# The input projection in float32 on unsplit operands, with a third weight buffer

## The chip, the cores and the metric

The kernel runs on one core of one Trainium2 chip. The metric is the device time of one execution in microseconds (us). The engines are TensorE (PE, with its weight loads shown as PEld), VectorE (DVE), ScalarE (ACT), GpSimd (POOL) and SyncE (SP), which issues most of the loads.

## The reference

One layer of a decoder computes 512 prompt tokens and a sample group of 8 x 4 tokens, 544 tokens in all, in float32:

```python
z = rms_norm(x, Wl['g_mix']) @ Wl['w_in']           # 1024 channels -> 3080 columns
za, zb, zc = jnp.split(z, [RWKV_COLS, RWKV_COLS + FOX_COLS], axis=-1)
ya, S, shift = rwkv7_mix(za, ...)                   # RWKV recurrence, 4 heads
q, k, v, logf = fox_project(zb, ...)                # FoX attention, 8 heads
yb = fox_fn(q, k, v, logf)
yc, conv_buf = conv_module(zc, ...)                 # 31 taps
x = x + jnp.concatenate([ya, yb, yc], axis=-1) @ Wl['w_out']
x = x + cross_attend(x, mk, mv, ...)
f, ffn_buf = conv_ffn(x, ffn0, ...)
x = x + f
```

The change concerns the first line, the input projection. The outputs are the new activations, the caches and the states.

## The kernel before

Activations lie with channels on the 128 partitions and the 544 tokens along a row, in eight blocks of 128 channels. A weight product takes a block of 128 output columns, a span of tokens (272, or 256 and 288 for the RWKV columns) and eight blocks k of the contraction, which add up in one bank of PSUM (`bank_g`, two of them).

Products take operands of type float32 or float32r, a type of the same size which keeps fewer digits. To keep the precision of float32 with float32r operands, each operand is split into a high and a low part, both float32r: `split` (L244) copies the high part on ACT (`w_hi`, L177) and takes the difference on DVE (`w_lo`, L247). `gemm_steps` (L306) then makes three products for each k: high x high, high weight x low activation, low weight x high activation. The activations are split once, where they come out of the first transposes (L481 and L482 make `act_h` and `act_l`); the weights are split block by block in `weights` (L267), just before use, with high priority.

Weights come through a pool of two slots (`wraw`, tile `w_raw`) of 2048 numbers on each partition, two blocks to a slot. SP issues the loads in order, each when its slot is free, which is when the split has read it. The same two slots take the first cached keys of the later attention, through GpSimd.

The stage has two parts. First come the eight blocks of RWKV columns, with the recurrence's gates beside them (`gates`, up to L673). Then `weave` (L1241) runs three streams side by side: the 17 other blocks (`fox_and_conv`: the forget gate, four of the convolution, twelve of FoX), the RWKV recurrence (`rwkv_recurrence`, ahead of the others by 800 instructions) and the convolution's taps (`conv_ahead`). `weave` takes the next step from the stream whose done share is least. A step of the projection counts `kb * n * 1.25e-3` of a total of 106, the recurrence counts to 79, the convolution to 84. When the projection ends, so does the weave; what is left of the other streams runs later beside the sample's attention. The recurrence ends with its sample steps (`sample_steps`), which load a state S (L971). Two pools of the stage close with the projection, and the attention's tiles take their place.

Of the kernel before, what the change touches and what calls it, by code (L numbers as in the profile page):

```python
# [43 lines left out]
def _consts():  # L44
    """What depends on shapes alone: identities, masks, selections."""
# [46 lines left out]
    # rows (head, page of four, query) against pages, queries and columns of the like  # L92
# [18 lines left out]
def _past_consts():  # L111
    """of rows (head, page of four, query): causal mask, selections of pages, queries and columns"""
# [14 lines left out]
def _cross_consts():  # L127
    """of rows (head of two, 64 of the keys, token) those of a head and the 64; then selections of 32 rows, four times over"""
    p, m = np.arange(128)[:, None], np.arange(8)[None, :]
    own = [(m // 4 == h) & (m % 4 == p // 32) for h in range(2)]  # L130
    four = [p == 32 * x + np.arange(128)[None, :] % 32 for x in range(4)]
    return np.concatenate(own + four, 1).astype(np.float32)
# [5 lines left out]
def _pack_vectors(x):  # L138
    """Per-channel vectors side by side, a column for each 128 channels."""
# [15 lines left out]
def hybrid_step(tc, A):  # L155
# [62 lines left out]
    def rsqrt_from(out, in_, scale, eps):  # L218
        """out = (in * scale + eps) ** -0.5 by the logarithm and the exponential"""
# [3 lines left out]
    def half_xyy(t, y, x, scale, eps):  # L223
        """t = (x * scale + eps) / 2 * y ** 2 for y, about the inverse root: (1.5 - t) * y is that root to the last bits"""
# [3 lines left out]
    def rsqrt_rows(out, x, n, scale, eps, eps_ap, work):  # L228
        """out = (x * scale + eps) ** -0.5 for n numbers to a partition"""
# [6 lines left out]
    def neg_sigmoid(t, e):  # L236
        """-1 / (1 + exp(-t)) in place, for t >= -40; by a Newton step"""
# [6 lines left out]
    def split(h, l, src, tt=vtt):  # L244
        """src = h + l exactly, both float32r"""
# [14 lines left out]

    wload = [nc.sync.dma_start]
# [5 lines left out]
    def weights(src, kb, cols, width=128, raws=None):  # L267
        """loads blocks of columns, two at most, and returns how to split each"""
# [13 lines left out]
        if raws is not None:  # L282
            raws.extend(parts)

# [21 lines left out]
    def gemm_steps(src, cols, xh, xl, evac, bank, spans=EVEN, kb=8, ahead=0, raws=None, first=None):  # L306
        """evac(ps, i, a) for span a of the i-th block of 128 columns; yields what each step costs TensorE"""
        for i0 in range(0, len(cols), at_once[0]):
            pair = cols[i0: i0 + at_once[0]]
            part = first if first and i0 == 0 else weights(src, kb, pair, raws=raws)  # L310
# [4 lines left out]
            for q, a in order:  # L315
                lo, n = spans[a]
                ps = bank()
                with tc.high_priority(ahead) if ahead else ExitStack():
                    for k in range(kb):
                        hv, lv = w[q](k)  # L320
# [3 lines left out]
                yield kb * n * 1.25e-3  # L324
# [1872 lines left out]
```

## Time and profile before

| | |
|---|---|
| time, median of 3 runs | 1304.64 us (1300.55 to 1308.29) |
| span of the profiled execution | 1301.6 us |
| PE, DVE, ACT, POOL busy | 95%, 62%, 39%, 22% of the span |
| the input projection's products | from 12.7 to 319.7 us |

Busy time is the time in which an engine has at least one instruction in flight. Products on PE are pipelined, so a busy PE is not PE at its peak. A row of a group gives a line of the kernel, engine, operation, output<-inputs, the shape, the number of instructions, their busy time and the mean duration of one, then the idle time of the engine just before them and what ended it. The granted clock is given as a share of 2.4 GHz.

### The profile page before, as it was taken

Reading aid. Unit: us, or ns where it says so; the run is one execution under the profiler, and the core shown is the slowest. Engines: PE = TensorE matmul, PEld = TensorE weight load, DVE = VectorE, ACT = ScalarE, POOL = GpSimd, SP = SyncE. Lnnn points to the kernel's source line nnn. Section 1 sums busy time; section 2 is a strip of 40 time slices with the busy share of each in tenths; the row PEclk is TensorE's granted clock in tenths of the full one; section 3 lists DMA queues with packets and bytes.
Section 4 is the critical chain, followed back from the end, with each engine's and each line's share of the span. In section 5 each row is a group of like instructions: output and inputs, shape, how many; then the busy total and the mean of one; then the engine's idle time right before and its main releaser. Section 6 shows DMA issues by size and latency. Waiting matters only on the chain.

```text
span 1301.6 us, 24852 instructions
## 1 busy us (share of the span) xinstructions
PE 1234.1 (95%) x10410; PEld 1011.6 (78%) x10410; DVE 809.1 (62%) x1514; ACT 501.2 (39%) x996; POOL 290.6 (22%) x322
## 2 busy tenths in 40 slices
PE   7899899999899999999998988999999999999997
PEld 6788788875555467654447875799999999999996
DVE  4699998765777377453234677557767424777631
ACT  5454543341456435221242422335444323444321
POOL 1262430033342131112223242012111100111120
PEclk9999999997699999999998998999999999999999
DMA  7221220221788497576663465033322323222231
GB/s 227 59 65 51 50 75 19 67 87 44 268 304 304 155 306 244 198 231 226 218 215 118 151 232 174 23 103 98 98 93 60 93 73 127 68 96 88 76 111 48
DMA packets 129649, 173.83 MB, mean 134 GB/s; under 512 B 7029, under 2 KB 110981, under 8 KB 121336
## 3 DMA queue, kind: packets, MB, share of 16 engines
q0 software_dynamic: 15216, 84.80, 18.1%
q1 hardware_dynamic: 88160, 70.76, 17.9%
q10 hardware_dynamic: 26160, 16.66, 4.4%
q8 instruction: 82, 1.34, 0.4%
q14 instruction: 31, 0.25, 0.1%
HBM read 164.54 MB, written 7.88 MB: 132 GB/s over the span
## 4 chain that ended last, share of the span: by engine, by line
PE 77%; DVE 9%; issue 5%; ACT 4%; DMA 3%; POOL 2%; SPq 0%; POOLq 0%; ACTq 0%; DVEq 0%
PE bank_g L186 42%; PE bank_r L186 10%; PE bank_d L186 6%; PE bank_s L186 6%; PE bank_v L186 4%; PE bank_a L186 2%; PE bank_r L216 2%; DVE w_lo L247 1%; PE bank_t L216 1%; PE bank_x L216 1%; DMA w_raw<-in_w_in_dram 1%; DMA w_raw<-in_w_out_dram 1%; DVE four L855 1%; DVE KT L1404 1%; ACT w_hi L177 1%
## 5 line engine op out<-in xcount | busy, mean ns | idle before, releaser
L186 PE MATMUL bank_g<-four,w_hi 128*128 128x272 f32 (+1 forms) x1536 | 284.7, 301 | 2.7 <-ACT w_hi L177 2.0
L177 ACT CAST w_hi<-w_raw 128x1024 fp32r<-128x1024 f32 (+3 forms) x149 | 140.6, 946 | 269.8 <-PE bank_g L186 206.1
L186 PEld LDWEIGHTS bank_g<-four,w_hi 128*128 128x128 f32 x1536 | 222.1, 189 | 26.4 <-issue 19.9
L247 DVE TENSOR_TENSOR w_lo<-w_raw,w_hi 128x1024 fp32r<-128x1024 f32 (+3 forms) x149 | 164.0, 1103 | 87.2 <-ACT w_hi L177 78.2
L186 PE MATMUL bank_g<-four,w_lo 128*128 128x272 f32 (+1 forms) x768 | 173.4, 301 | 0.5 <-DVE w_lo L247 0.5
L186 PEld LDWEIGHTS bank_g<-four,w_lo 128*128 128x128 f32 x768 | 122.1, 189 | 11.3 <-issue 8.6
L186 PE MATMUL bank_g<-act_h,w_hi 128*128 128x272 f32 (+2 forms) x400 | 124.6, 312 | 6.2 <-ACT w_hi L177 2.8
L186 PE MATMUL bank_g<-act_h,w_lo 128*128 128x272 f32 (+2 forms) x400 | 122.9, 308 | 0.0
L186 PE MATMUL bank_g<-act_l,w_hi 128*128 128x272 f32 (+2 forms) x400 | 122.0, 305 | 0.0
L2108 POOL TENSOR_SCALAR ysm<-HS,vec 128x32 f32<-128x32 f32 x44 | 42.0, 954 | 255.1 <-ACT HS L177 255.1
L1404 DVE STREAM_TRANSPOSE KT<-w_raw 128x2048 f32<-128x2048 f32 x32 | 73.5, 2302 | 23.9 <-PE bank_s L186 22.8
L186 PEld LDWEIGHTS bank_g<-act_h,w_hi 128*128 128x128 f32 x400 | 79.5, 199 | 10.5 <-ACT w_hi L177 3.2
L186 PEld LDWEIGHTS bank_g<-act_h,w_lo 128*128 128x128 f32 x400 | 79.1, 198 | 2.8 <-issue 1.2
L186 PEld LDWEIGHTS bank_g<-act_l,w_hi 128*128 128x128 f32 x400 | 79.4, 198 | 2.3 <-issue 1.1
L186 PE MATMUL bank_s<-KT,w_hi 128*32 128x128 f32 x1024 | 76.6, 292 | 3.4 <-DVE rsq L226 1.7
L186 PE MATMUL bank_d<-four,w_hi 128*128 128x272 f32 x384 | 78.1, 299 | 0.0
L186 PE MATMUL bank_g<-in_h,w_hi 128*128 128x272 f32 x352 | 73.6, 290 | 0.0
L186 PE MATMUL bank_g<-in_l,w_hi 128*128 128x272 f32 x352 | 73.5, 290 | 0.0
L186 PE MATMUL bank_g<-in_h,w_lo 128*128 128x272 f32 x352 | 73.2, 289 | 0.0
L186 PE MATMUL bank_v<-page,w_lo 128*32 128x512 f32 x256 | 67.8, 603 | 1.8 <-DMA page<-in_cache_fox_v_dram,kidx 1.8
L186 PEld LDWEIGHTS bank_s<-KT,w_hi 128*32 128x32 f32 x1024 | 39.2, 115 | 32.5 <-issue 19.8
L186 PEld LDWEIGHTS bank_d<-four,w_hi 128*128 128x128 f32 x384 | 61.9, 193 | 1.0
(631 smaller groups left out, 2458.6 us busy)
## 6 DMA issues: line engine op xcount, KB each, us to landing
w_raw<-in_w_up_dram SPq DMA_DIRECT2D x20, 1024.0 KB, 5.1
w_raw<-in_w_down_dram SPq DMA_DIRECT2D x16, 704.0 KB, 4.7
w_raw<-in_w_in_dram SPq DMA_DIRECT2D x17, 512.0 KB, 4.2
w_raw<-in_cache_mem_k_dram SPq DMA_DIRECT2D x16, 512.0 KB, 5.0
sV<-in_cache_mem_v_dram POOLq DMA_DIRECT2D x12, 512.0 KB, 6.4
w_raw<-in_w_in_dram SPq DMA_DIRECT2D x4, 1024.0 KB, 6.6
w_raw<-in_w_xk_dram ACTq DMA_DIRECT2D x8, 512.0 KB, 10.6
w_raw<-in_w_xv_dram ACTq DMA_DIRECT2D x8, 512.0 KB, 10.7
```

The costliest lines, as they stand in the source:

```text
L177: nc.scalar.copy(out, in_)
L186: pinned(nc.tensor.matmul(out, lhsT, rhs, start=start, stop=stop, skip_group_check=True))
L216: pinned(nc.tensor.transpose(out=out, in_=in_, identity=ident[p0:p0 + k, p0:p0 + k]))
L247: tt(out=l, in0=src, in1=h.bitcast(F32), op=SUB)
L855: vstt(out=yp, in0=U[:, m, w: w + SEQ], scalar=w_tap, in1=yp, op0=MUL, op1=ADD)
L1404: nc.vector.transpose(out=KT, in_=K)
L2108: nc.gpsimd.tensor_scalar(out=ysm, in0=H[:, 2:6, 1:], scalar1=w[2], scalar2=b, op0=MUL, op1=ADD)
```

## The change

The projection's operands are no longer split. `xh` holds the scaled activations once, as float32; half of the copies that fill it move from ACT to DVE. The tile `act_l` goes, and in its place a pool `wmore` adds a third slot to the rotation of weight slots for this stage. `weights` hands out the raw tile, and `gemm_steps` makes one float32 product for each k when there is no low activation. The planner counts such a step 1.67e-3 for each k and column in place of 1.25e-3; the totals in `weave` stay. All other weight products remain split. The rest of the diff removes comments and moves the class `Slots` up.

```diff
+    class Slots:
+        def __init__(self, *pools):
+            self.turns, self.n = [p for p, k in pools for _ in range(k)], -1
+        def tile(self, *args, **kw):
+            self.n += 1
+            return self.turns[self.n % len(self.turns)].tile(*args, **kw)
...
-    def weights(src, kb, cols, width=128, raws=None):
+    def weights(src, kb, cols, width=128, raws=None, whole=False):
...
+        if whole:
+            return lambda i: lambda k: (parts[i][:, k],)
...
-            part = first if first and i0 == 0 else weights(src, kb, pair, raws=raws)
+            part = first if first and i0 == 0 else weights(src, kb, pair, raws=raws, whole=xl is None)
...
                     for k in range(kb):
+                        if xl is None:
+                            mm(ps[:, :n], w[q](k)[0], xh[k][:, lo: lo + n], k == 0, k == kb - 1)
+                            continue
                         hv, lv = w[q](k)
...
-                yield kb * n * 1.25e-3
+                yield kb * n * (1.25e-3 if xl else 1.67e-3)
...
-    xh, xl = (acts.tile([128, 8, NT], F32R, name=n) for n in ("act_h", "act_l"))
+    wslot[0] = Slots((wraw, 2), (pool("wmore", 1, axs), 1))
+    xh = acts.tile([128, 8, NT], F32, name="act")
...
-            early = weights(A["w_in"][0], 8, [m * 128 for m in order_z[:2]])
+            early = weights(A["w_in"][0], 8, [m * 128 for m in order_z[:2]], whole=True)
...
-                h, l = xh[:, m, lo: lo + n], xl[:, m, lo: lo + n]
-                act(out=h, in_=p, func=AF.Copy, scale=V("g_mix", m))
-                vstt(out=l, in0=p, scalar=V("g_mix", m), in1=h.bitcast(F32), op0=MUL, op1=SUB)
+                if m % 2:
+                    vts(out=xh[:, m, lo: lo + n], in0=p, scalar1=V("g_mix", m), scalar2=None, op0=MUL)
+                else:
+                    act(out=xh[:, m, lo: lo + n], in_=p, func=AF.Copy, scale=V("g_mix", m))
...
-    for step in gemm_steps(w_in, [m * 128 for m in order_z], blocks(xh), blocks(xl), evac_z, gb, spans=((0, 256), (256, 288)), first=early):
+    for step in gemm_steps(w_in, [m * 128 for m in order_z], blocks(xh), None, evac_z, gb, spans=((0, 256), (256, 288)), first=early):
...
     def fox_and_conv():
-        x = blocks(xh), blocks(xl)
+        x = blocks(xh), None
...
     axs.close()
+    wslot[0] = wraw
```

## Rows read from the trace of the kernel before

**Rows 1.** The page: busy time by engine, and the granted clock in 40 slices.

```profile
PE 1234.1 (95%) x10410; PEld 1011.6 (78%) x10410; DVE 809.1 (62%) x1514; ACT 501.2 (39%) x996; POOL 290.6 (22%) x322
...
PEclk9999999997699999999998998999999999999999
```

**Rows 2.** Busy time by engine and stretch; the last three are clock, DMA, GB/s.

```profile
core 0: us, PE busy (x) PEld busy (x) DVE busy (x) ACT busy (x) POOL busy (x), PEclk, DMA share, GB/s
12.00:62.00 50.00, 44.48 (x300) 40.92 (x300) 30.64 (x60) 22.95 (x43) 9.58 (x18) 0.97 0.39 117
62.00:178.00 116.00, 105.58 (x810) 97.20 (x810) 111.25 (x193) 58.65 (x86) 51.09 (x51) 0.96 0.25 64
178.00:250.00 72.00, 71.76 (x1179) 60.89 (x1179) 60.29 (x151) 24.95 (x64) 6.24 (x8) 1.00 0.11 31
250.00:320.00 70.00, 69.71 (x568) 51.00 (x565) 40.43 (x93) 24.64 (x57) 18.63 (x19) 0.90 0.23 63
```

**Rows 3.** Groups by line, 12 to 320 us: one pass's products, weight loads.

```profile
L186 PE MATMUL bank_g<-act_h,w_hi 128*128 128x272 f32 (+2 forms) x400 | 124.6, 312 | 6.2 <-ACT w_hi L177 2.8 <-DVE fsq L816 1.3 <-DVE zS L565 1.0
...
L186 PEld LDWEIGHTS bank_g<-act_h,w_hi 128*128 128x128 f32 x400 | 79.5, 199 | 10.5 <-ACT w_hi L177 3.2 <-issue 2.1 <-DVE fsq L816 1.2
```

**Rows 4.** Timeline: start, length; first and last of 43 back-to-back float32r products.

```profile
275.73 0.29 PE L186 MATMUL bank_g<-act_h,w_lo 128*128 128x272 f32 x1
...
281.01 0.29 PE L186 MATMUL bank_g<-act_h,w_lo 128*128 128x272 f32 x1
```

**Rows 5.** Chain of waits, 12 to 320 us, shares by line.

```profile
by line: PE bank_g L186 26.9%; PE bank_r L186 25.9%; DVE w_lo L247 4.0%; issue 3.5%; PE bank_x L216 3.0%; DVE four L855 3.0%; PE bank_r L216 2.8%; PE bank_x L186 2.0%; DVE Dr L954 1.9%; DVE later L523 1.6%; DVE zb L575 1.2%; DVE zb L576 1.1
```

**Rows 6.** Timeline: a float32r product, then four records of float32 products.

```profile
264.73 0.29 PE L186 MATMUL bank_g<-act_h,w_lo 128*128 128x272 f32 x1
264.85 1.08 PE L186 MATMUL bank_x<-fsq,cf 128*128 128x272 f32 x4
```

**Rows 7.** Groups by line, 62 to 178 us: products of one pass.

```profile
L186 PE MATMUL bank_g<-act_h,w_hi 128*128 128x272 f32 (+2 forms) x205 | 62.4, 304 | 3.4 <-DVE fsq L816 1.3 <-DVE zS L565 1.0 <-DVE X L955 0.4
```

**Rows 8.** Groups by line: the splits up to 320 us, then 62 to 178.

```profile
L177 ACT CAST w_hi<-w_raw 128x1024 fp32r<-128x1024 f32 x25 | 26.1, 1046 | 33.2 <-PE bank_g L186 32.4 <-DMA w_raw<-in_w_in_dram 0.8
...
L247 DVE TENSOR_TENSOR w_lo<-w_raw,w_hi 128x1024 fp32r<-128x1024 f32 x25 | 31.7, 1271 | 3.5 <-ACT w_hi L177 3.5
...
L247 DVE TENSOR_TENSOR w_lo<-w_raw,w_hi 128x1024 fp32r<-128x1024 f32 x13 | 17.1, 1318 | 0.0
```

**Rows 9.** PE's waits, 12 to 320 us: total, times, longest.

```profile
PE bank_x L186 <- DVE ft L226: 3.6, 1, 3.6
PE bank_g L186 <- ACT w_hi L177: 2.8, 1, 2.8
```

**Rows 10.** Busy time and clock, columns as in rows 2: the dips.

```profile
155.00:160.00 5.00, 1.74 (x11) 1.13 (x9) 5.00 (x8) 2.93 (x7) 3.58 (x2) 0.88 0.00 0
160.00:165.00 5.00, 4.67 (x18) 4.43 (x19) 5.00 (x10) 3.36 (x7) 2.61 (x3) 0.50 0.00 0
305.00:310.00 5.00, 5.00 (x14) 1.50 (x9) 1.59 (x6) 0.22 (x2) 0.99 (x1) 0.50 0.18 41
```

**Rows 11.** The same at 400 to 450 us, and its first group on PE.

```profile
400.00:450.00 50.00, 49.45 (x359) 25.69 (x359) 27.67 (x73) 26.72 (x80) 11.15 (x11) 1.00 0.65 233
...
L186 PE MATMUL bank_s<-KT,w_hi 128*32 128x128 f32 x138 | 12.0, 281 | 0.0
```

**Rows 12.** The low activations: durations in ns, smallest, median, largest.

```profile
L482 DVE SCALAR_TENSOR_TENSOR act_l<-bank_r,vec,act_h x8: 474/495/518, 8.6 to 22.2; 128x256 fp32r<-128x256 f32 x4, 128x288 fp32r<-128x288 f32 x4
```

**Rows 13.** The page's loads of the projection's weights; timeline of SP's queue.

```profile
w_raw<-in_w_in_dram SPq DMA_DIRECT2D x17, 512.0 KB, 4.2
...
254.53 1.83 SPq L971 DMA_DIRECT2D S<-in_state_rwkv_dram  x2
```

**Rows 14.** Timeline: first and last products of the recurrence's sample steps on PE.

```profile
281.23 1.15 PE L186 MATMUL bank_r<-ident,S 64*64 64x64 f32 x32
...
312.62 0.48 PE L216 MATMUL bank_r<-ident,y 128*128 128x128 f32 x1
```

More of the change, by code (lines that the diff above doesn't have):

```diff
@@ L1615, in normed @@
         vstt(out=l, in0=xTs[m // 4][:, m % 4, s], scalar=V("g_x", m), in1=h.bitcast(F32), op0=MUL, op1=SUB)
-    class Slots:
-        def __init__(self, *pools):
-            self.turns, self.n = [p for p, k in pools for _ in range(k)], -1
-        def tile(self, *args, **kw):
-            self.n += 1
-            return self.turns[self.n % len(self.turns)].tile(*args, **kw)
     def slot():
```

## The prediction

> **What bounds the kernel now.** I read the page first: the span has TensorE (PE) busy 95%, and the line of granted clock shows where it ran below full speed [rows 1]. That 95% is a mean over stages, so next comes the busy time by stretch [rows 2]. The projection's products run from 12 to 320 us. The reader is to see three regimes there. Until 62 us nothing is full. From 62 to 178 VectorE (DVE) is busy 111.25 of 116 us and PE 105.58. From 178 to 320 PE is busy 141.5 of 142 us, and DVE has room. So PE's visible idle time is 5.5 us before 62, 10.4 between 62 and 178, and 0.5 behind, 16.4 in all. The mean clock costs more: 0.03 x 50, 0.04 x 116, 0 and 0.10 x 70 us make 1.5 + 4.6 + 7 = 13.1.
>
> Then the groups by line: each of the three passes (high x high, high weight x low activation, low weight x high activation) has 400 products [rows 3], so there are 400 sums of a block, a span and a k. Their pace is read from the starts in the timeline: 42 steps of 128x272 from 275.73 to 281.01 us are 0.1257 us each [rows 4]. (The duration of 0.29 us is latency.) The chain of waits says the same as the regimes: in this stretch the projection's banks hold 26.9%, the recurrence's 25.9%, the split's low half (w_lo) 4.0% [rows 5].
>
> **The change, part by part.**
>
> *Products.* 1200 products in float32r become 400 in float32 on the same tiles. The trace of before has such float32 products of 128x272: each appears as two records. Four records start behind a float32r product that ends at 264.73 + 0.29 = 265.02 us, and end at 264.85 + 1.08 = 265.93: 0.91 / 4 = 0.2275 us a record, 0.455 us a product [rows 6]. Three passes of 0.1257 take 0.377 us. The spans of 256 and 288 columns come in pairs and have the mean of 272. So PE gets 400 x (0.455 - 0.377) = +31 us of streaming. By stretch: 205 of the 400 lie between 62 and 178 us [rows 7]; by the same count 75 lie before, 39 from 178 to 250 and 81 behind. That is +21.8 us before 178 and +9.4 behind.
>
> *Splits removed.* 25 copies to w_hi on ScalarE (ACT) of 1.046 us and 25 differences to w_lo on DVE of 1.27 us go: 26 us of ACT, 32 of DVE, 17.1 of these between 62 and 178 [rows 8]. What they free on the path is not these 32 us but the time that PE waited: at the start 2.8 us for the first w_hi, and otherwise waits for DVE's chains, the longest 3.6 us [rows 9]; DVE's order is shared, so fewer splits shorten these. Of 15.9 us of idle before 178 I take two thirds as recovered, 10.5, because DVE falls there from 111 to some 94 of 116 us and PE, filled by the longer products, is then the fuller engine; the bounds are 0 and 15.9. Behind 178 there is next to nothing to recover.
>
> *Clock.* Two dips matter. From 155 to 165 us PE idled while DVE was busy 5.00 of 5.00, and the clock fell to 0.50 [rows 10]; with less on DVE this dip should shrink. From 305 to 310 the clock is also at half (1.2 of 2.4 GHz), with PE busy 5.00 of 5.00 us: there run the 32-row products of the recurrence's sample steps. Of the 6.1 us lost before 178 I take 2.5 back, of the 7 behind 178 half, 3.5; bounds 0 and 13.1. Float32 itself keeps the clock: from 400 to 450 us, with float32 products of the cached keys as the largest group, it is 1.00 [rows 11].
>
> *Activations.* 8 of the 16 scaled copies go from ACT to DVE in place of 16 differences of 0.495 us [rows 12]. Both engines get lighter before 25 us; PE waits there for loads as well. I put it at 0, the first wait above being already counted; if DVE's copies came late, each would cost 0.5.
>
> *Loads and the third buffer.* A slot is now free when its last product has run, no longer when it is split. A pair of blocks is four steps of 8 products, 4 x 8 x 0.455 = 14.6 us, and a load lands after 4.2 us [rows 13]: with three slots the next pair is loaded a pair ahead. Cost 0, hidden under 14.6 us; without that cover 4.2 us in each of 15 turns. Behind a waiting load on SyncE's queue stand the small loads of the RWKV stage and, behind the last one, the recurrence's state S, asked for at 254.53 us right after the projection's last load [rows 13]. On GpSimd two loads of cached keys wait for the same slots, with the sample steps' products of masks behind them.
>
> *Planner.* A step now counts 8 x 272 x 1.67e-3 = 3.6 in place of 2.7, in a total left at 106. 34 steps come to 1.17 of it, before to 0.87, so the recurrence and the taps are asked for sooner and the end is projection alone. No work is added: 0, apart from the dip at 305 us above.
>
> *Sum.* Before 178 us: 21.8 - 10.5 - 2.5 = +8.8. Behind: 9.4 - 3.5 = +5.9. Together +14.7. The profiled execution's own span is 1301.6 us and gives 1316.3; the median of the runs shown, 1304.64, lies 3.0 above it, and on that I forecast 1319.3. The bounds: everything recovered, 31.2 - 15.9 - 13.1 = +2.2, 1306.8; nothing recovered, +31.2, 1335.8.
>
> **The rivals.**
>
> *DVE led, faster.* Between 62 and 178 us DVE is full, and w_lo stands in the chain of waits [rows 2, 5]. If DVE's order alone sets when the recurrence starts (178 us), the 13 splits bring it 17.1 us earlier; behind 178 stand +9.4 and up to -7 of clock. The time would be 1304.6 - 17.1 + 9.4 - 3.5 = 1293. Against it: it decides only if PE's work in the stretch fits. Products alone go from 205 x 0.377 = 77 to 93 us, of 116 - 17 = 99, and the other 195 records there must find place in 6.
>
> *All absorbed, no change.* Idle and clock both come back whole: 1306.8, by the lower bound. For it: DVE's relief lies where PE idles. Against: 16.4 us of idle stand in front of +31.
>
> *Nothing absorbed, slower still.* The waits are of single chains (ft, zb, dp) that need their PE results first; these come 20% later. 1335.8. If the float32 record takes 0.24 us, as with a drain at every change of tile shape, 400 x (0.48 - 0.377) = +41, 1346.
>
> *The slot held too long, slower.* The state S is loaded only when the last projection load has its slot, now 8 steps (29 us) before the end. The sample steps' products took from 281.23 to 312.62 us [rows 14]; begun 4.2 us after that load they would end some 7 us behind the projection, and ACT's and GpSimd's part 3 more. That adds at most 10 to the forecast: 1329.
>
> *Weight loads set the pace, faster.* Each product loads its own weights, and a load lasts 0.199 us in the records [rows 3]. There were 1200 and will be 800. If loads were not hidden behind products, 400 fewer would give -80 us and the sum -49, 1256. Against it: 0.1257 us from start to start is less than one load, so they overlap [rows 3, 4]. The Trainium skill, "TensorE: Matmul & The Clock Gate", Part 3, on what overlaps, says that a weight load overlaps running products only where the row groups differ. By that rule the loads of all 128 rows would stand bare; the trace does not agree, with 0.126 against 0.199 us.
>
> That a float32 product would run in one pass, as the old ones, is excluded by the two records [rows 6].
>
> **How the numbers follow.** Forecast (+8 to +24) 0.55; nothing absorbed 0.11; slot held 0.05; all absorbed 0.16; DVE led 0.11; weight loads 0.02. A measurement of this kernel can tell about 0.5%, 6.5 us. So slower 0.71, same 0.16, faster 0.13. The likeliest gives 1319. The range is to hold it 8 times in 10: from 1298, which leaves out the greater part of the two faster cases, to 1338, which leaves out the dearer record and a part of what combines.
>
> **What would show it.** 400 records of PE fewer; 25 each of w_hi and w_lo gone; records of 128x272 at 0.227 us from start to start. The projection's last product comes some 15 us later than 320 us. PE stays full from 178 on, DVE from 62 to 178 falls by 17 us, and the dip at 155 to 165 us shrinks. Wrong would be: the recurrence's first products well ahead of 178 us with the end of the projection ahead of 320 (DVE led), idle PE waiting for w_raw (the slots), or a clock at half while float32 products run back to back.

## The result and the profile after

The changed kernel takes 1337.61 us (median of 4 runs, 1333.33 to 1338.31); the kernel before, on the same chip, 1303.14. The ratio is 1.0255, 95% interval 1.0228 to 1.0282: 34.5 us slower. The forecast was 1319 with a range to 1338, so it had the sign and not the size: +34.5 where it added up +14.7. The profiled execution has a span of 1335.9 us against 1301.6, +34.3.

From the page of the changed kernel, TensorE's busy time and the granted clock, to set beside [rows 1]:

```profile
PE 1268.3 (95%) x10010; PEld 995.7 (75%) x10010; DVE 775.6 (58%) x1479; ACT 475.5 (36%) x965; POOL 274.8 (21%) x322
...
PEclk9999898989989999999998999999999999999998
```

The 400 records fewer are there, DVE lost 33.5 us and ACT 25.7. PE's busy time rose by 34.2 us, as much as the span. Busy time by stretch, columns as in [rows 2]:

```profile
62.00:178.00 116.00, 105.60 (x959) 82.55 (x957) 86.92 (x190) 31.71 (x59) 29.18 (x42) 0.94 0.15 38
178.00:250.00 72.00, 67.39 (x766) 51.40 (x762) 57.86 (x128) 23.33 (x58) 11.98 (x13) 0.95 0.16 40
12.00:62.00 50.00, 46.63 (x216) 35.76 (x217) 29.19 (x63) 23.67 (x39) 6.87 (x14) 1.00 0.38 116
250.00:320.00 70.00, 69.41 (x386) 44.56 (x382) 28.99 (x68) 17.17 (x40) 21.43 (x21) 0.93 0.30 79
```

Between 62 and 178 us DVE fell from 111.25 to 86.92 us, and PE is busy 105.60 where it was 105.58: none of its 10.4 us of idle time was filled. Ahead of 62 us, 2.2 of its 5.5 us went. Behind 178, where PE had been full, 4.6 us of idle and a clock of 0.95 are new. The pace of the new products is as forecast. Timeline, start and length:

```profile
336.65 7.50 PE L186 MATMUL bank_g<-act,w_raw 128*128 128x272 f32 x32
343.99 1.08 PE L186 MATMUL bank_x<-fsq,cf 128*128 128x272 f32 x4
```

32 records in 343.99 - 336.65 = 7.34 us are 0.229 us each, against 0.2275 in [rows 6]. The projection's last product starts at 348.3 us (319.5 before), 28.8 us later, so most of the +34.3 is there when the projection ends.

Far behind the projection, two groups that the change does not touch took longer. They are the sample's score products (KT) and value products (page). Each writes 32 output rows, one of four strips, and is called a strip product below. Groups by line over the whole span, kernel before:

```profile
L186 PE MATMUL bank_s<-KT,w_hi 128*32 128x128 f32 x1024 | 76.6, 292 | 3.4 <-DVE rsq L226 1.7 <-DVE st L1424 1.2 <-DVE KT L1404 0.3
L186 PE MATMUL bank_v<-page,w_lo 128*32 128x512 f32 x256 | 67.8, 603 | 1.8 <-DMA page<-in_cache_fox_v_dram,kidx 1.8
```

And the changed kernel:

```profile
L186 PE MATMUL bank_s<-KT,w_hi 128*32 128x128 f32 x1024 | 82.4, 291 | 4.8 <-DVE KT L1422 4.7
L186 PE MATMUL bank_v<-page,w_lo 128*32 128x512 f32 x256 | 78.0, 630 | 3.9 <-DMA page<-in_cache_fox_v_dram,kidx 3.9
```

Together 144.4 against 160.4 us. The number of records is the same, and so is the mean duration of one, nearly; what differs is how many were in flight side by side.

**A ledger of the span.** In slices of 5 us I multiply PE's busy time by the granted clock; the sum is the *work*, the time that PE would have been busy at full clock. Busy time less work is the *clock loss*, and the rest of the span is *idle*. Before: 1201.0 + 33.1 + 67.5 = 1301.6. After: 1243.6 + 24.7 + 67.6 = 1335.9. So the +34.3 is +42.6 of work, -8.4 of clock loss and +0.1 of idle. Of the work, 31.2 is the forecast's price of the float32 products, the strip products' busy time gives +16.0, and the remainder of -4.6 is put down to all other groups together. Up to the projection's last product the difference is +25.7 of work, +0.7 of clock loss and +2.5 of idle; behind it, +16.9, -9.0 and -2.5. The experiments ask why the idle time stayed, and where the 16 us come from.

### The profile page after: what moved, and what is told of

Same layout as the page of the kernel before. It is cut to its first block, busy times and chain, and to the rows that moved or that the text cites. A ratio compares the mean times of both kernels' runs of the same rounds, so it can differ in the third digit from the quotient of the medians.

```text
span 1335.9 us, 23967 instructions
## 1 busy us (share of the span) xinstructions
PE 1268.3 (95%) x10010; PEld 995.7 (75%) x10010; DVE 775.6 (58%) x1479; ACT 475.5 (36%) x965; POOL 274.8 (21%) x322
## 4 chain that ended last, share of the span: by engine, by line
PE 63%; issue 5%; DVE 4%; DMA 3%; POOL 2%; ACT 2%; POOLq 0%; DVEq 0%; ACTq 0%
PE bank_g L186 37%; PE bank_s L186 7%; PE bank_d L186 6%; PE bank_v L186 5%; PE bank_r L186 3%; PE bank_r L216 2%; PE bank_a L186 1%; DMA page<-in_cache_fox_v_dram,kidx 1%; PE bank_t L216 1%; DVE KT L1422 1%; PE bank_k L216 1%; DMA w_raw<-in_cache_fox_k_dram,kidx 1%; DMA w_raw<-in_w_xq_dram 0%; ACT w_hi L177 0%; DVE w_lo L247 0%
## 5 line engine op out<-in xcount | busy, mean ns | idle before, releaser
L186 PEld LDWEIGHTS bank_g<-four,w_hi 128*128 128x128 f32 x1536 | 221.5, 188 | 23.8 <-issue 20.4
L186 PE MATMUL bank_g<-act,w_raw 128*128 128x272 f32 (+2 forms) x800 | 213.6, 414 | 4.4 <-DMA w_raw<-in_w_in_dram 4.2
L177 ACT CAST w_hi<-w_raw 128x1024 fp32r<-128x1024 f32 (+2 forms) x124 | 114.5, 925 | 240.3 <-PE bank_g L186 190.6
L186 PEld LDWEIGHTS bank_g<-act,w_raw 128*128 128x128 f32 x800 | 151.5, 197 | 40.0 <-issue 8.2
L247 DVE TENSOR_TENSOR w_lo<-w_raw,w_hi 128x1024 fp32r<-128x1024 f32 (+2 forms) x124 | 133.5, 1079 | 79.0 <-ACT w_hi L177 62.3
L1422 DVE STREAM_TRANSPOSE KT<-w_raw 128x2048 f32<-128x2048 f32 x32 | 73.5, 2303 | 30.9 <-PE bank_s L186 23.5
L186 PE MATMUL bank_s<-KT,w_hi 128*32 128x128 f32 x1024 | 82.4, 291 | 4.8 <-DVE KT L1422 4.7
L186 PE MATMUL bank_v<-page,w_lo 128*32 128x512 f32 x256 | 78.0, 630 | 3.9 <-DMA page<-in_cache_fox_v_dram,kidx 3.9
L186 PEld LDWEIGHTS bank_s<-KT,w_hi 128*32 128x32 f32 x1024 | 39.5, 114 | 35.8 <-issue 18.3
L1407 POOL DMA_INDIRECT page<-in_cache_fox_v_dram,kidx x32 | 32.9, 1029 | 134.7 <-PE bank_v L186 124.6
L186 PE MATMUL bank_g<-xT,w_hi 128*128 128x256 f32 x256 | 58.1, 308 | 0.0
L2109 DVE TENSOR_TENSOR up<-bank_g,tot 128x544 f32<-128x544 f32 x44 | 31.8, 722 | 44.6 <-PE bank_g L186 44.6
L186 PE MATMUL bank_d<-four,w_lo 128*128 128x272 f32 x192 | 56.5, 294 | 0.0
```

The costliest lines, as they stand in the source:

```text
L177: nc.scalar.copy(out, in_)
L186: pinned(nc.tensor.matmul(out, lhsT, rhs, start=start, stop=stop, skip_group_check=True))
L247: tt(out=l, in0=src, in1=h.bitcast(F32), op=SUB)
L1407: nc.gpsimd.indirect_dma_start(out=t, out_offset=None, in_=A[cache][0].rearrange("n (k j) h d -> (n k) (j h d)", j=4), in_offset=bass.Indi ...
L1422: nc.vector.transpose(out=KT, in_=K)
L2109: vtt(out=two(x[:, 2:]), in0=ev2(ps), in1=two(rstd), op=MUL)
```

## The experiments

"Switches" in this table are counted in the program's order of TensorE's instructions: two neighbouring products (transposes too) of which just one has fewer than 128 output rows. The strip column is the busy time of the two groups above. The ratio is to the runs of the kernel before on the same chip. Work, idle and clock loss are of one profiled execution each, not always one near the median: those of b_group and b_g800 lie 6 us under it, b_hi_thrice's 8 under and a_group's 8 above.

| kernel | median us | ratio, 95% interval | switches | strips | work | idle | clock loss |
|---|---|---|---|---|---|---|---|
| before | 1304.6 | 1 | 607 | 144.4 | 1201.0 | 67.5 | 33.1 |
| after | 1337.6 | 1.0255 (1.0228 to 1.0282) | 647 | 160.4 | 1243.6 | 67.6 | 24.7 |
| a_weave | 1339.5 | 1.0276 (1.0247 to 1.0304) | 625 | 155.8 | 1235.5 | 68.3 | 28.3 |
| a_two_slots | 1329.1 | 1.0192 (1.0132 to 1.0252) | 581 | 141.0 | 1221.6 | 79.5 | 24.4 |
| a_early_k | 1334.7 | 1.0233 (1.0201 to 1.0265) | 647 | 158.4 | 1243.6 | 66.2 | 23.4 |
| a_splits_kept | 1338.2 | 1.0279 (1.0234 to 1.0325) | 645 | 158.9 | 1242.9 | 72.5 | 16.2 |
| b_hi_thrice | 1295.1 | 0.9930 (0.9907 to 0.9952) | 607 | 142.7 | 1198.6 | 67.8 | 18.9 |
| b_hi_once | 1229.5 | 0.9433 (0.9396 to 0.9470) | 367 | 121.5 | 1039.0 | 137.2 | 52.1 |
| b_extra | 1326.4 | 1.0144 (1.0106 to 1.0181) | 605 | 148.6 | 1233.3 | 68.6 | 23.2 |
| b_group | 1252.3 | 0.9585 (0.9545 to 0.9626) | 373 | 87.9 | 1125.9 | 78.3 | 40.5 |
| a_group | 1290.3 | 0.9896 (0.9853 to 0.9939) | 385 | 103.0 | 1163.8 | 80.3 | 52.4 |
| a_two_slots_g | 1290.1 | 0.9876 (0.9841 to 0.9912) | 385 | 94.7 | 1161.1 | 85.6 | 41.8 |
| b_hi_thrice_g | 1245.7 | 0.9542 (0.9507 to 0.9578) | 373 | 86.8 | 1125.3 | 82.5 | 35.5 |
| b_g800 | 1258.3 | 0.9633 (0.9596 to 0.9669) | 345 | 82.7 | 1123.8 | 90.0 | 36.8 |
| a2_g800 | 1270.6 | 0.9743 (0.9697 to 0.9790) | 315 | 84.0 | 1144.7 | 88.0 | 35.8 |
| b_extra_g800 | 1266.2 | 0.9705 (0.9663 to 0.9748) | 337 | 84.7 | 1153.0 | 86.8 | 24.6 |
| b_hi_thrice_g800 | 1244.3 | 0.9522 (0.9479 to 0.9564) | 345 | 81.6 | 1119.6 | 87.0 | 31.8 |
| a_g200 | 1285.2 | 0.9831 (0.9793 to 0.9868) | 355 | 91.2 | 1160.4 | 88.4 | 34.5 |
| b_extra50_g800 | 1339.5 | 1.0247 (1.0212 to 1.0281) | 473 | 86.3 | 1185.8 | 84.8 | 67.6 |
| b_extra100_g | 1401.4 | 1.0742 (1.0684 to 1.0800) | 537 | 85.0 | 1255.0 | 82.5 | 62.1 |

Runs of one kernel scatter by about 4 us either way, and the clock loss of one profile with them, so little is built on single differences under some 6 us.

**1. The planner's weight (a_weave).**

```diff
-                yield kb * n * (1.25e-3 if xl else 1.67e-3)
+                yield kb * n * 1.25e-3
```

> The changed kernel with one number put back: a projection step is costed to the weave at 1.25e-3 per column and k block, as before the change, and not at 1.67e-3. Theory A (the stretch to the projection's end is set by TensorE's own work plus waits inside the recurrence's chain, which go wherever the chain goes): 1334 to 1341, the same as the changed kernel within 0.3%; the projection's end moves later relative to the recurrence, the idle moves but stays near 19 us. Theory B (the dearer weight brought the recurrence forward, and this spent the relief of VectorE): 1315 to 1328.

1339.5 against 1337.6: no difference. The recurrence still begins as early (its first XS,beta product at 145.7 us, 150.1 in the changed kernel, 191.8 before). Theory B falls.

**2. Slots (a_two_slots, a_early_k).** The first takes the third slot away, the second adds a fourth and frees the two shared ones early:

```diff
-    wslot[0] = Slots((wraw, 2), (pool("wmore", 1, axs), 1))
+    wslot[0] = wraw
```

> The changed kernel without the third weight buffer: the projection's loads take turns in two slots, as before the change. Theory A (weights are never late): 1335 to 1341, no change within 0.3%. Theory C (with no split between, a slot is held until its last product, and two slots are too few): 1343 to 1355, with TensorE waiting for weight loads. Theory D (the third slot is what delays the first cached keys): 1328 to 1334.

```diff
-    wslot[0] = Slots((wraw, 2), (pool("wmore", 1, axs), 1))
+    wmore = pool("wmore", 2, axs)
+    wslot[0] = Slots((wraw, 2), (wmore, 2))
+    wslot[0].turns = [wraw, wraw, wmore, wmore, wraw, wraw, wmore, wmore, wraw, wraw, wmore, wmore, wmore, wmore, wmore]
```

> The changed kernel with a fourth weight slot in the freed place, and the projection's last five loads take turns in the two added slots alone, so that the two slots which the cached keys also use come free some 45 us before the projection ends instead of at its end. Theory D (cached keys asked for too late after the change: TensorE idle 360 to 368 and a late first tile): 1327 to 1332, 6 to 10 us below the changed kernel. Theory A: the time is set elsewhere and the 7 us come back as another wait: 1334 to 1340.

The first gives 1329.1, the range that theory D had named, the second 1334.7, theory A's. Waits in the changed kernel from 12 to 360 us, in total, times and longest:

```profile
POOL w_raw L1407 <- PE bank_g L186: 20.1, 2, 10.3
PE bank_g L186 <- DMA w_raw<-in_w_in_dram: 4.2, 1, 4.2
```

Weights were late once, at the very start, and the two loads of cached keys did wait for slots, as the prediction had named them. But with the slots free early (first key load at 242.8 us and not 324.0) the time stays within the scatter, and the first KT product moves only from 357.5 to 355.7: theory D's reason falls. Yet without the third slot the kernel was some 8 us faster (its runs reach from 1321 to 1337, so this is little more than the scatter), although the keys came later still (339.1 us). What is clear of the scatter is the order: the third slot changed where the scheduler placed the strip products, 581 switches against 647, and they took 160.4 us where they had 141.0. The run with two slots was idle for 12 us more.

**3. VectorE's relief (a_splits_kept, b_hi_thrice, b_hi_once).** The first puts the splits back beside the float32 products, unused. The other two, from the kernel before, drop `w_lo` and `act_l`:

```diff
-            return lambda i: lambda k: (parts[i][:, k],)
+            def kept(i):
+                hi = wsplit[0].tile([128, 8, 128], F32R, name="w_hi")[:, :kb, :width]
+                lo = wsplit[0].tile([128, 8, 128], F32R, name="w_lo")[:, :kb, :width]
+                with tc.high_priority():
+                    split(hi, lo, parts[i][:, :kb])
+                return lambda k: (parts[i][:, k],)
+            return kept
```

> The changed kernel with the weight splits put back but used by nothing: 25 ScalarE copies to w_hi and 25 VectorE subtractions to w_lo run ahead of each block as before the change, the products still read the unsplit weights in float32. So VectorE and ScalarE have nearly the load of before and TensorE that of after. Theory A (VectorE's relief is worth nothing): 1335 to 1341. Theory E (the relief was worth the 10 to 13 us which the forecast counted on and something else took them): 1346 to 1353.

```diff
-                        for n_pass, (wv, x) in enumerate(((hv, xh), (hv, xl), (lv, xh))):
+                        for n_pass, (wv, x) in enumerate(((hv, xh),) * 3 if xl is None else ((hv, xh), (hv, xl), (lv, xh))):
```

> The kernel before with the input projection's low parts left out, and TensorE's load kept: each of the 400 places still has three float32r products, but all three of the high parts. Left out are 25 VectorE subtractions (w_lo, 1.27 us each by the rows of before, 32 us in all, 16.5 of them between 12 and 178) and the activations' 16 low parts. This is VectorE's relief alone, with the weave, the slots and TensorE's work of before. Theory A (VectorE does not set the time in 12 to 178, the idle there is latency of the recurrence's and the gates' chain): 1297 to 1305. Theory E (VectorE led there): 1285 to 1293.

> As the run with the high parts thrice, but each place has one float32r product only: 800 products of 0.126 us are left out, 100 us of TensorE's work. It asks what sets the time when TensorE's share goes. Theory A (TensorE's work adds one for one until something else binds): 1200 to 1230. Theory E (VectorE or the chain of the gates and the recurrence is close behind in 12 to 178, 111 of 116 us busy before): 1240 to 1275.

The stretch from 62 to 178 us, columns as above; b_hi_thrice:

```profile
62.00:178.00 116.00, 105.43 (x1142) 96.25 (x1142) 106.92 (x216) 56.58 (x90) 46.50 (x48) 0.97 0.19 49
```

a_splits_kept:

```profile
62.00:178.00 116.00, 105.44 (x936) 82.60 (x934) 97.22 (x197) 39.70 (x65) 32.03 (x43) 0.97 0.15 38
```

b_hi_once:

```profile
62.00:178.00 116.00, 63.07 (x445) 49.61 (x445) 107.17 (x202) 58.81 (x97) 49.60 (x49) 0.68 0.18 49
```

With DVE busy 111, 107, 97 or 87 us, PE's idle time in this stretch is 10.4, 10.6, 10.6 and 10.4 us. So the 24 us by which DVE's load differs did not set it. Giving the splits back costs the changed kernel nothing (theory A). The relief alone saved 9.4 us, between the ranges of theories A and E, but not as idle time: in the ledger of its profiled execution, the shortest of its runs, idle is +0.3 us and the clock loss -14.2, of which 9 lie behind the projection. With a third of the products, PE is idle for 53 us here, and DVE is busy in 49 of them; the idle time in all is twice what it was, and 100 us of products less bring 75 (theory A's range). So DVE is the second bound and stands close behind, but not in front.

**4. The order of the strip products (b_group, a_group, a_two_slots_g, b_hi_thrice_g).** One edit, in a place that has nothing to do with the projection, gives the strip products a priority, so that the scheduler places those of a page next to each other; the same is done around the value products. A run is a stretch of neighbours of one group in TensorE's queue.

```diff
-            for x in range(4):
-                for hp, po in enumerate(QUAD):
+            for x, hp, po in ((x, hp, po) for x in range(4) for hp, po in enumerate(QUAD)):
+                with tc.high_priority(60):
                     mm(acc[po, pg * 128: (pg + 1) * 128], ...
```

> The kernel before, with one thing added far from the change: the sample's score products (KT, 1024 records) and value products (page, 256 records) get a priority of 60 instructions, so that the 16 (or 4) products of a page, which lie on four strips of 32 rows, stand in TensorE's queue in 36 and 33 runs and not in 138 and 62. Theory F (products of different strips run side by side only where they stand next to each other; in the trace of before these two groups take 76.6 and 67.8 us, of the changed kernel 82.4 and 78.0, with 160 and 72 runs): four side by side would take 1024 x 0.273 / 4 = 70 and 256 x 0.603 / 4 = 39 us, so up to 35 us less: 1270 to 1290. Rival G (the cached pages' transfers or VectorE's transposes set the pace of this stage, and TensorE then only waits): 1297 to 1308.

> The changed kernel with the same priority: 45 and 42 runs and not 160 and 72. Theory F (part of the 34.5 us is the other order of these products and not the projection): the changed kernel gains some 8 us more from it than the kernel before does, so 1288 to 1312, and the distance between the two with it is 24 to 29 us. Theory A (the distance is the projection's own): the distance stays 32 to 37 us.

> The same, and without the third weight buffer. Without the priority that buffer cost 8 us, and two slots had 131 and 63 runs where three had 160 and 72. Theory F: with the priority both have nearly the same runs (42 and 39; 45 and 42), so two slots and three agree within 4 us. Theory D (the third buffer itself costs, by when the slots come free): two slots stay 6 to 10 us faster.

> The kernel before with the same priority, and the projection's low parts left out as in the run with the high parts thrice (VectorE relieved of 25 subtractions and the activations' low parts, TensorE's load kept): VectorE's relief alone, under the same order of the sample's products (36 and 33 runs with it and without). If the 9 us that the relief gave without the priority are the projection's: 7 to 12 us below the kernel before with the priority. If they were the clock at the start of the sample's attention (0.66 between 320 and 360 before, 0.91 with the relief), which another order may hold up anyway: 0 to 4 us below it.

The kernel before becomes 51 us faster (1252.3, 4.1%), more than theory F had dared: both strip groups fall below its estimate of 70 and 39 us in sum, to 87.9. This version beats both kernels, the changed one by 85 us. Two slots and three now agree to 0.2 us, at 385 switches both, so here the third slot costs nothing; part 6 has a case where it may. But the distance between the changed kernel and the kernel before became 38 us and not 24 to 29, a little over theory A's 32 to 37: there theory F is wrong, or not enough. The relief gives 6.6 us, between its two expectations.

How the order costs is seen in the timeline. The changed kernel, start and length:

```profile
501.22 0.58 PE L186 MATMUL bank_g<-xT,w_hi 128*128 128x256 f32 x2
501.74 0.41 PE L186 MATMUL bank_s<-KT,w_hi 128*32 128x128 f32 x2
502.07 0.38 PE L186 MATMUL bank_g<-xT,w_lo 128*128 128x256 f32 x1
502.38 0.41 PE L186 MATMUL bank_s<-KT,w_hi 128*32 128x128 f32 x2
502.72 0.38 PE L186 MATMUL bank_g<-xT,w_hi 128*128 128x256 f32 x1
```

And the kernel before with a priority of 800 (b_g800):

```profile
500.07 0.40 PE L186 MATMUL bank_g<-xT,w_hi 128*128 128x256 f32 x2
500.31 0.28 PE L186 MATMUL bank_g<-xT,w_lo 128*128 128x256 f32 x1
...
505.94 1.06 PE L186 MATMUL bank_s<-KT,w_hi 128*32 128x128 f32 x26
506.93 0.50 PE L186 MATMUL bank_g<-xT,w_hi 128*128 128x256 f32 x2
```

In turn, a KT product (two records) and a full product take 502.38 - 501.74 = 0.64 us, at a granted clock of 1.00. Among their like they take 0.08 (thirteen KT products in 506.93 - 505.94 = 0.99, since those of different strips run side by side) and 0.12 (two full ones in 500.31 - 500.07 = 0.24): 0.20 in sum. So two switches cost 0.44 us, 0.22 each, and PE is counted busy all the while. In that figure are the switch itself and what a strip product loses that has no other beside it; the two were not separated. The same from the whole: 234 switches fewer and 51.1 us, 0.22 each. The type changes at such a switch too (KT's products are float32, two records each, xT's float32r, one), but in [rows 6] float32 products follow a float32r one after 264.85 - 264.73 = 0.12 us, float32r's own pace, so that change of type, in one shape, adds nothing. The Trainium skill, "TensorEngine Tiling (Array Packing)", Key Properties, says that changing the tiling mode drains the engine while tiles of one mode run in parallel; the trace agrees that a switch costs time, 0.22 us, and that the strips run side by side, but doesn't show whether the engine is drained.

**5. The order held (b_g800, a2_g800, b_extra_g800, b_hi_thrice_g800).** A priority of 800 brings the strip products into 33 and 31 runs, in all four to within one. The control b_extra adds to the kernel before about the work that float32 adds, and relieves nothing:

```diff
-                        for n_pass, (wv, x) in enumerate(((hv, xh), (hv, xl), (lv, xh))):
+                        more = ((lv, xl),) if extra[0] and k < 5 else ()
+                        for n_pass, (wv, x) in enumerate(((hv, xh), (hv, xl), (lv, xh)) + more):
```

> The kernel before with the priority of the sample's products raised from 60 to 800 instructions: 33 and 31 runs in TensorE's queue (36 and 33 with 60), nearly the 32 and 32 pages. As fast as with 60 or a little faster: 1244 to 1254. It is the base for the three beside it, which have the same runs to within one.

> The changed kernel without the third weight buffer, with the same priority: 34 and 32 runs. With 60 this kernel had 42 and 39 runs and stood 38 us above the kernel before with the priority, though the projection's products alone add 31.2. Theory F (the rest is still the order of the sample's products): 27 to 34 us above its base. Theory I (the float32 products themselves cost more than their pace, by the clock: 20 to 21 us of clock loss ahead of 350 with them, 15 without): 36 to 42 us above its base.

> A control: the kernel before (splits, float32r) with the same priority, and in 5 of 8 blocks of k a fourth product, low parts by low parts: 250 products more of 0.126 us, 31.4 us of TensorE's work, about what float32 adds, and no relief of VectorE or ScalarE. Theory A (TensorE's work adds one for one): 29 to 34 us above its base, and the changed kernel is no better than this control, or by the relief's 0 to 7 us. Theory E (VectorE's load set the stretch to 178, and 21.8 us of added TensorE work would there hide behind it): 10 to 22 us above its base.

> VectorE's relief alone (the projection's low parts left out, TensorE's load kept), with the same priority and the same 33 and 31 runs as its base. With 60 it stood 6.6 us below. Theory A: 0 to 4 us below its base. Theory E: 6 to 12 us below.

The strips now agree (82.7, 84.0, 84.7, 81.6 us). The base itself missed its expectation: 1258.3 us, 6 slower than b_group with 28 switches fewer, so the count doesn't tell all. Float32 costs 12.3 us, the control 8.0, both less than any theory had; the relief alone gives 14.0, more than theory E had. In the ledger, idle moves by -2.0, -3.2 and -3.0 us in these three: even here nothing to speak of. The control's 29.2 us of work are paid for by 12.2 less of clock loss (its profiled span is 13.8 above its base's). Float32 got no clock back (-1.0), but has 30 switches fewer than its base.

The times of the projection's last product tell where these sums arise. It starts at 319.1 us in b_g800, at 349.1 in a2_g800, 342.6 in the control and 319.0 with the relief. So, as far as these times tell, float32 costs 30.0 us up to there, nearly its 31.2 of products, the control 23.5, and the relief brings 0.1; what makes the sums small lies behind the projection. Much of that is clock. The kernel before and b_g800 lose some 8 us of clock in the 20 us behind the projection, the changed kernel 0.6 and the two controls 1.9 and 1.1. Busy time in the first 10 or 20 of these, kernel before:

```profile
320.00:330.00 10.00, 7.11 (x30) 4.80 (x28) 8.38 (x24) 1.99 (x9) 7.73 (x10) 0.63 0.75 244
330.00:340.00 10.00, 10.00 (x120) 6.40 (x122) 5.54 (x7) 4.02 (x10) 4.38 (x5) 0.50 0.60 189
```

changed kernel:

```profile
350.00:360.00 10.00, 9.75 (x159) 6.24 (x159) 7.85 (x19) 4.30 (x15) 8.44 (x12) 1.00 0.89 296
```

Since the control has it too, and a_group, with float32, loses 7.3 us there, this gain belongs neither to float32 nor to the relief.

**6. The whole change, the control without priority, and larger doses (a_g200, b_extra, b_extra50_g800, b_extra100_g).** The last two take the fourth product in all 8 blocks of k, then twice.

> The changed kernel whole, third weight buffer included, with a priority of 200 for the sample's score and value products: 35 and 35 runs in TensorE's queue, where the changed kernel has 160 and 72 and, with a priority of 60, has 45 and 42. Theory F (the order of the strip products took the rest): 1266 to 1280, within 8 us of the same without the third buffer (1270.6, 34 and 32 runs). Theory D (the third buffer costs by itself): 1280 to 1290.

> The control without any priority: the kernel before with a fourth product in 5 of 8 blocks of k (250 more, 31.4 us of TensorE's work), nothing relieved; 141 and 65 runs of the strip products against 138 and 62 before. Theory A (the added work goes one for one): 1332 to 1338. Theory J (about three quarters of it are absorbed, as where the order was held fixed, 8.0 us of 31.4): 1309 to 1320.

> A larger dose of the control, priority 800, 32 and 31 runs: a fourth product in all 8 blocks of k, 400 products more, 50.3 us of TensorE's work. Base 1258.3, with 31.4 us more 1266.2. If about 23 us are absorbed and the rest goes one for one: 1282 to 1290. If the share absorbed is the same: 1268 to 1274. One for one from the first: 1305 to 1311.

> A larger dose still: a fourth and a fifth product in all blocks of k, 800 products more, 100.6 us of TensorE's work, priorities of 200 and 100, 35 and 34 runs. If about 23 us are absorbed and the rest goes one for one: 1330 to 1342. If the share absorbed is the same: 1280 to 1290. One for one from the first: 1353 to 1363.

The whole change stands at 1285.2, 27 us above b_g800, in theory D's range and not within 8 us of the two-slot one (1270.6) as theory F had it; it has 40 switches more than that, at 0.22 us each 9 us, of which 7 show in the strip column. The priority differs too, so whether the third slot costs something by itself here stays open. The control without priority costs 18.7 us: its 1326.4 lies between J's 1309 to 1320 and A's 1332 to 1338, with 9.9 us of clock loss given back. The doses contradict every line that I had drawn: 31.4 us of added products cost 8.0 us, 50.3 cost 81, 100.6 cost 143. The table shows where it goes: with 400 products more the scheduler dealt the projection one by one between the recurrence's products, 473 switches against 345 in b_g800, and of the 87.6 us between the two profiled spans 62.0 are work and 30.8 clock loss. Timeline of b_extra50_g800:

```profile
263.32 0.47 PE L186 MATMUL bank_r<-tok,G 64*64 64x64 f32 x2
263.72 0.59 PE L186 MATMUL bank_g<-act_h,w_lo 128*128 128x272 f32 x1
264.25 0.47 PE L186 MATMUL bank_r<-WU,G 64*64 64x64 f32 x2
...
268.05 0.43 PE L186 MATMUL bank_g<-act_h,w_hi 128*128 128x272 f32 x1
268.27 0.43 PE L186 MATMUL bank_g<-act_l,w_hi 128*128 128x272 f32 x1
```

and its busy time from 260 and from 290 us:

```profile
260.00:270.00 10.00, 10.00 (x36) 7.15 (x36) 1.08 (x2) 0.37 (x1) 0.00 (x0) 0.50 0.01 2
290.00:300.00 10.00, 10.00 (x96) 9.25 (x95) 8.90 (x20) 2.24 (x5) 2.59 (x3) 1.00 0.48 133
```

A 64x64 product and a product of the projection in turn take 264.25 - 263.32 = 0.93 us, with PE busy 10.00 of 10 us and the clock at half; the projection's product takes 0.22 us among its like at the same clock and 0.126 at full [rows 4].

**All runs together.** A least-squares line through the 19 kernels without b_hi_once, drawn after the fact, gives for the difference to the kernel before: 0.195 us for each switch, 1.10 us for each us of added products, -2.3 us for the relief, and -6 us at nothing, with a root mean square error of 5.8 us. It misses b_extra_g800 by 15 us, b_g800 and b_extra by 10, and by its -6 at nothing the kernel before itself; what it misses was not traced to a cause. b_hi_once doesn't fit (it would come out at -166 and measures -75), since PE is no longer the bound there. By this line the change is +34 for its products, +8 for 40 switches and -2 for the relief, less 6; being fitted to the change among others, it describes and doesn't prove.

## Why the prediction was wrong in size

*The sign, the bound and the price of the products: right.* Records of 0.229 us, 400 fewer, PE still the bound. The measured 1337.6 lies just inside the range to 1338, but the change is more than twice the forecast's +14.7: three parts of the sum were off. The control (8 to 19 us) and the doses show that added work on PE is paid for, though not by its pace alone.

*The step that failed first: "Of 15.9 us of idle before 178 I take two thirds as recovered, 10.5, because DVE falls".* DVE fell more than forecast (24 us against 17) and PE's idle time between 62 and 178 us did not move (10.4 both times). Of the 15.9 us ahead of 178, 2.2 came back, all ahead of 62 us. Even the wait at the start stayed: where PE had waited 2.8 us for the first w_hi [rows 9], it now waits 4.2 for the load itself, once. The stretch was read as two engines that compete, since both were nearly full [rows 2], so that any load taken from DVE would shorten PE's waits. But it matters what DVE does while PE waits. Laid over each other, the records show DVE busy in all of the 10.4 us in the kernel before, but with w_lo in only 1.4 of them and with the stage's other steps in the rest; in the changed kernel it is busy in 9.7 of 10.4. Once the old waits were gone, others stood in their place. The changed kernel's groups from 62 to 178 us with the most idle time before them:

```profile
L186 PE MATMUL bank_r<-RA,beta 64*64 64x64 f32 (+1 forms) x112 | 7.0, 255 | 2.1 <-DVE G L1113 2.1
L186 PE MATMUL bank_r<-rt,cf 128*128 128x272 f32 x16 | 4.3, 399 | 3.8 <-DVE rt L664 3.8
L186 PE MATMUL bank_r<-zbuf,G 64*64 64x64 f32 x32 | 3.3, 274 | 2.5 <-DVE zbuf L1120 2.5
```

The second of these in the timeline, start and length:

```profile
64.36 1.54 PE L186 MATMUL bank_r<-rt,cf 128*128 128x272 f32 x6
65.05 3.46 DVE L242 SCALAR_TENSOR_TENSOR rt<-rt,rt 128x1088 f32<-128x1088 f32 x1
68.77 2.46 DVE L641 TENSOR_TENSOR_SCAN rt<-tap,rt 128x544 f32<-128x544 f32 x2
71.14 0.41 DVE L664 TENSOR_SCALAR rt<-bank_r 128x272 f32<-128x272 f32 x1
71.61 0.73 PE L186 MATMUL bank_r<-rt,cf 128*128 128x272 f32 x2 [3.77 <-DVE rt L664]
```

The step that PE waits for (L664) reads products that ended at 65.90 us; it starts at 71.14, behind other steps in DVE's queue. So the rival of nothing absorbed was right that the idle time stays, but its reason, single chains that wait for PE's results, isn't the reason of this wait.

G and zbuf belong to the recurrence. A row of the changed kernel's tile XS dates its start:

```profile
L186 PE MATMUL bank_r<-XS,beta x56: 218/218/366, 150.1 to 235.8; 64*64 64x64 f32 x56
```

Before it began at 191.8 us. The prediction had named this ("the recurrence's first products well ahead of 178 us") as one half of the sign that DVE led and the time falls; the other half, an end of the projection ahead of 320, did not come. The recurrence came earlier, and brought its own waits along: 4.6 us of idle appear from 178 to 250, where there had been 0.24. It moved forward with the splits kept as well (157.4), with the relief alone (159.8) and with the control (173.7), so which edit moves it is not settled.

*The second: the clock, of which 2.5 us were to come back ahead of 178 and 3.5 behind.* Up to the projection's end nothing came back: the mean clock by stretch costs 0 + 7.0 + 3.6 + 4.9 = 15.5 us where it had cost 13.1. The half clock that had stood at 305 us under the sample steps came with them, at 275 to 280 us. What came back (8.4 us in the ledger) lies behind the projection, in a stretch that the prediction had not looked at: 15.0 us of clock loss from 320 to 700 us before, 8.2 from 350 to 735 after, most of it right behind the last product (part 5). That the total came near the forecast's 6 us is luck. It is also of the size by which the clock loss varies between two executions with nearly the same order ahead of 350 us (13.5 in the changed kernel, 20.4 in a_group).

*What the sum lacked: the order of what comes later.* The prediction put loads and third buffer at "Cost 0". That held for the loads (the wait at the start apart, PE never waited for weights) and not for the order: with the third buffer the strip products stand in another order, 647 switches where two slots have 581 and the kernel before 607, and take 160.4 us where these have 141.0 and 144.4. The prediction had a drain "at every change of tile shape" in one rival, at 10 us and for the projection's own products; a cost of such changes showed 300 us further on.

*Slots and planner.* Neither the slot held too long nor the dearer step cost anything that could be measured (a_early_k, a_weave).

*Rivals.* "Nothing absorbed", 1335.8, lies nearest, but for half a reason: idle wasn't absorbed, as it said; the clock gave 8 us back and the order took 16. How much float32 would cost in all with everything else fixed stays open: 12 us (a2_g800 over b_g800), 27 (a_g200 over the same) and 38 (a_group over b_group). Corrected by the count of switches, at 0.22 us, they are 19, 25 and 35. But up to the projection's last product the three pairs agree, 30.0, 28.7 and 31.3 us, as does the change itself with 28.8: there float32 costs its products, with little absorbed. What differs arises behind the projection. The clock loss against the base (-1.0, -2.3 and +11.9 us) accounts for a part of the third, whose profile lies 8 us above its median; the rest was not separated.

## What to carry to other kernels

Two engines that are both nearly full needn't compete: before relief of one is credited to the other's idle time, look at what it does in the idle moments themselves (here, splits in 1.4 of 10.4 us), then take the load away alone and see whether the idle time moves. Price a matrix product by its neighbours in the queue as well as by its columns: a narrow and a full product in turn took three times what they take in groups, and a busy engine doesn't show it. Where a scheduler deals the instructions, any edit can reorder a stage far away, so count such switches in both programs before the difference is put down to the edit; grouping them here was worth 51 us, more than the change cost.

## What the runs showed of the hardware

A switch between a product on 32 output rows and one on 128 costs 0.22 us at full clock (0.64 us for a pair that takes 0.20 in groups), the lost overlap of the strips included. With 64-row products in turn with full ones the pair takes 0.93 us while the granted clock is 0.50 and PE is busy 10.00 of 10 us: the clock was at its lower level although the engine was never idle in the records, and it was back at 1.00 from 290 us, with 96 records in 10 us where there had been 36. Which of the two, order or clock, brought the other isn't shown. And the 1024 records of KT, grouped, keep PE busy for 39.7 us (b_g800), 0.039 us each, where theory F had reckoned 0.273 / 4 = 0.068: the duration of a record is mostly latency, here as in [rows 4], so a quarter of it is no floor for four strips side by side.
